# Opening of a two-layer diffusion block: small parameters ahead of X, squares on two engines, their sums on TensorE

## The chip, the cores and the metric

The kernel runs on one core of a Trainium2 chip. TensorE (PE; its weight loads are listed as PEld), VectorE (DVE), ScalarE (ACT) and GpSimd (POOL) each work through an instruction list of their own; SyncE (SP) issues the transfers. The metric is device microseconds of one execution; three executions of the kernel before took 1885.79, 1888.84 and 1891.24 us, so 1888.84 in the median.

## What is computed

A backbone of two layers over 512 latent tokens with 256 context tokens, width 1024. Layer 0 mixes tokens with grouped-query attention, layer 1 with a bidirectional Mamba-2 scan, and each is followed by a gated convolutional FFN. Each sub-layer starts like this (`c` conditions the latent tokens, `c_ctx` the context):

```python
silu_c = jax.nn.silu(c)
mod_l = jnp.split((silu_c @ ada_w[i] + ada_b[i])[:, None, :], 6, axis=-1)
# rms_norm(x, g) = x * rsqrt(mean(x * x, -1) + EPS) * g
h_l = rms_norm(x, norm_mix_w[i]) * (1 + mod_l[1]) + mod_l[0]
q_l, k_l, v_l = jnp.split(h_l @ w_qkv, [Q_DIM, Q_DIM + KV_DIM], axis=-1)
```

The change touches only the first of these, layer 0 ahead of attention: the silu of `c`, the sum of squares of every token, and the first products with `w_qkv`.

## The kernel before

X is kept with the width on the partitions: 8 row blocks (m = 0 to 7) of 128 x 512 latent columns and 128 x 256 context columns. A product of f32 exactness is made of three products of two-part operands (`mm3`, L105, L106, L108: high weights by high input, high by low, low by high). PE therefore needs for each block m a weight slab (`wst`, cast to `wsh` by ACT and reduced to the low part `wsl` by POOL) and a modulated input in two parts (`hha` by ACT, `hla` by DVE, both from `ht`).

The order on PE, ACT and DVE is the written order of the function `attention` (a manual schedule); SP issues in written order too. A transfer can be issued only when one of eight places is free.

The opening, in the names of the profile:

- `body` issues four transfers of X (L1562, two blocks each) and then all parameters (`par`, 548 columns, L1563). `attention` issues the weights of the first modulation (`wada`, in `ada`, L123, three transfers for each m), the slab (L544), the constants `cst` (L553) and so on up to m = 4.
- `busy(n)` makes n products of a matrix of ones with itself (`warm`, L565); nothing reads them.
- ACT squares the eight blocks (`sql`, L571), DVE adds them up in `acc` (L573), and `rstd_rows` lets PE sum over the partitions with four one-column products (`ssa`, L275), then makes the reciprocal root on DVE and ACT (`rsa` L279, `rsy` L281, `rsu` L283 and L284, `rba` L287) and turns it round on PE (`rsTa`, L293).
- `ada` of block m has three parts: issue the weights; eight products of the silu by the weights (`ps_ada`, L129) and their copy to SBUF (`ada_sb`, L131); two products that turn that copy round (`ps_adt`, L135) and the modulation on DVE (`mod` L146, `moda` L149). `modulated` then makes `ht` (L322), `hha` (L331) and `hla` (L332).
- The main loop runs over m. For each m there are six output groups (`k_step`, j = 0 to 5), three products each, into six PSUM accumulators `ps_l`. Within the groups of block m the second part of ada for m + 1 comes ahead of j = 0, its third part and the modulated input of m + 1 after j = 1. For m = 1 and 2 ACT squares four context blocks each and DVE adds them (`sqc`, L612 and L614).

Of the kernel before, what the change touches and what calls it, by code (L numbers as in the profile page):

```python
# [28 lines left out]
PC = {}  # L29
_n = 0  # L30


def _col(name, n):
    global _n
    PC[name] = _n
    _n += n


for _i in range(2):
    _col(f"nmix{_i}", KT)  # L40
    _col(f"nffn{_i}", KT)
    _col(f"adab{_i}", 6 * KT)
    for _t in range(3):
        _col(f"fw{_i}{_t}", NFT)
    _col(f"fb{_i}", NFT)
# [4 lines left out]
_col("snw", 16)  # L50
_col("alog", 1)
_col("dtb", 1)
_col("cc", 2 * KT)
_col("qn", 1)
_col("kn", 1)
NPAR = _n

CST_IDENT, CST_BLK, CST_SEL, CST_COS, CST_SIN = 0, 128, 130, 132, 132 + L
# [9 lines left out]
def t3(g, name, dt=F32, n=T):  # L68
    return g.t3p.tile([P, n], dt, tag="t3", bufs=g.n3, name=name)


def t4(g, name, dt=F32):
    return g.p.tile([P, 1024], dt, tag="t4", bufs=10, name=name)
# [35 lines left out]
    return i  # L109


def ada(g, src, layer, chunks, m0, nm, big=True):


    nc = g.nc
    cols = nm * len(chunks) * P
    per = (1024 if big else T) // cols
    st = []
    for k0 in range(0, KT, per):
        n = min(per, KT - k0)  # L120
        t = t4(g, "wada") if big else t3(g, "wada")
        t = t[:, : n * cols].rearrange("p (k a b) -> p k a b", k=n, a=len(chunks))
        nc.sync.dma_start(t.rearrange("p k a b -> p (k a b)"), src[:, k0 * cols : (k0 + n) * cols])  # L123
        st += [t[:, k].rearrange("p a b -> p (a b)") for k in range(n)]
    yield 0
    ps = Bank(g, "ps_ada")
    for k in range(KT):
        j = k % 4
        nc.tensor.matmul(ps[32 * j : 32 * j + 32, 0:cols], g.sc32[:, k, :], st[k], start=k < 4, stop=k >= 4)  # L129
    sb = g.t3p.tile([P, 512], F32, tag="t2", bufs=6, name="ada_sb")  # L130
    nc.vector.tensor_copy(sb[:, 0:cols], ps[:, 0:cols])  # L131
    yield BREAK
    pt = Bank(g, "ps_adt")
    for i in range(cols // P):
        nc.tensor.matmul(pt[:, 2 * i : 2 * i + 2], sb[:, i * P : (i + 1) * P], g.sel, start=True, stop=True)  # L135
    for i, ch in enumerate(chunks):
        modulation(g, pt[:, 2 * nm * i : 2 * nm * (i + 1)].rearrange("p (m v) -> p m v", v=2), layer, ch, m0, nm)
    yield BREAK
# [124 lines left out]
    follow(g, g.nc.scalar.preload_act_table_set("natural_log_exp_and_others"))  # L263


def rstd_rows(g, sq, n, cols, width, name, bank, behind=lambda: None):

    nc = g.nc  # L270
    c = cols.shape[-1]
    nt = n // P
    ps = bank(f"ss{name}")
    for t in range(nt):
        i = nc.tensor.matmul(ps[:, t * c : (t + 1) * c], sq[:, t * P : (t + 1) * P], cols, start=True, stop=True)  # L275
        ordered(g, i, behind())
    small = lambda nm: g.p.tile([P, nt * c], F32, tag="rst", bufs=8, name=nm)
    a, y, u = small("rsa"), small("rsy"), small("rsu")
    nc.vector.tensor_scalar(a, ps[:, : nt * c], 1.0 / width, EPS, ALU.mult, ALU.add)  # L279

    for f in ((lambda: nc.scalar.activation(y, a, AF.Ln)), (lambda: nc.scalar.activation(y, y, AF.Exp, scale=-0.5))):  # L281
        follow(g, f()) if g.tables else f()
    nc.vector.tensor_tensor(u, y, a, ALU.mult)  # L283
    nc.vector.scalar_tensor_tensor(u, y, -0.5, u, ALU.mult, ALU.mult)  # L284
    rb = t3(g, f"rb{name}", n=n)
    wide = lambda v: v.unsqueeze(2).broadcast_to([P, nt * c, P // c])
    nc.vector.scalar_tensor_tensor(rb.rearrange("p (a b) -> p a b", b=P // c), wide(u), 1.5, wide(y), ALU.add, ALU.mult)  # L287
    yield BREAK
    out = []
    for t0 in range(0, nt, 4):  # L290
        pt = bank(f"rsT{name}")
        for t in range(t0, min(nt, t0 + 4)):
            i = nc.tensor.transpose(pt[:, (t - t0) * P : (t - t0 + 1) * P], rb[:, t * P : (t + 1) * P], g.ident)  # L293
            ordered(g, i, behind())
        yield (pt, t0 * P, min(n, (t0 + 4) * P))
# [55 lines left out]
def Bank(g, name):  # L351
    return g.ps.tile([P, 512], F32, tag="B", bufs=4, name=name)
# [159 lines left out]
def attention(g, adas, project, X):  # L512


    nc, I = g.nc, g.I
    S64 = slice(0, 64), slice(64, 128)
    Bk, Sb = (lambda name: Bank(g, name)), (lambda name: S(g, name))
    t2 = lambda name, dt=F32: g.t3p.tile([P, 512], dt, tag="t2", bufs=6, name=name)
# [4 lines left out]
    ET = mybir.EngineType  # L523
    man = g.tc.manual_schedule(engines={ET.PE, ET.Activation, ET.DVE})
    man.__enter__()
    mods = [ada(g, I["adaA"][m], 0, (0, 1), m, 1, big=False) for m in range(KT)]
    W6 = 6 * P

    slabs = []
# [18 lines left out]

    loads = [slab() for _ in range(KT)]
    xs = [[X[:, m, c0:c1] for m in range(KT)] for c0, c1 in ((0, L), (L, T))]  # L550
    next(mods[0])
    next(loads[0])
    nc.sync.dma_start(g.cst, I["cst"][:, :CST_COS])  # L553
    for m in range(1, 5):
# [8 lines left out]
    def busy(n):  # L563
        for _ in range(n):
            nc.tensor.matmul(warm[:, :P], g.ones, g.ones, start=True, stop=True)  # L565

    busy(38)
    acc = t3(g, "acc", n=L)
    for m in range(KT):
        sq = t2("sql") if m else acc  # L570
        nc.scalar.activation(sq, xs[0][m], AF.Square)  # L571
        if m:
            nc.vector.tensor_tensor(acc, acc, sq, ALU.add)  # L573
    norm = rstd_rows(g, acc, L, g.ones[:, :1], D, "a", Bk)
    g.qn8 = g.const.tile([P, 1], F32, name="qn8")
    nc.vector.tensor_scalar(g.qn8, g.par[:, PC["qn"] : PC["qn"] + 1], -0.5 / HD * HD ** -0.5, None, ALU.mult)
    kn = g.const.tile([P, 1], F32, name="kn")
    nc.vector.tensor_scalar(kn, g.par[:, PC["kn"] : PC["kn"] + 1], -0.5 / HD, None, ALU.mult)

    e = g.p.tile([P, 2 * KT], F32, name="silu")  # L580
    nc.scalar.activation(e, g.cin, AF.Exp, scale=-1.0)
    nc.vector.tensor_scalar(e, e, 1.0, None, ALU.add)
    nc.vector.reciprocal(e, e)
    nc.vector.tensor_tensor(g.sc32[:, :, 0:2], g.cin.rearrange("p (k v) -> p k v", v=2),
                            e.rearrange("p (k v) -> p k v", v=2), ALU.mult)
    next(norm)
    next(mods[0])
    busy(8)
    rsl, _, _ = next(norm)
    next(mods[0])  # L590
    next(loads[0], None)
    busy(3)
    modulated(g, hl[0], xs[0], rsl, 0, L, 0, 1, 0, 0, 0)
    rs_ps, rsl = rsl, t3(g, "rsl", n=L)
# [8 lines left out]
    for m in range(KT):  # L603
        if 1 <= m < KT - 5 + 1:
            next(mods[m + 5 - 1])
            next(loads[m + 5 - 1])
        if m == 1:
            sqc = t3(g, "sqc", n=C)
        if m in (1, 2):
            for a in range(4 * m - 4, 4 * m):  # L610
                sq = t2("sqc")[:, :C] if a else sqc
                nc.scalar.activation(sq, xs[1][a], AF.Square)  # L612
                if a:
                    nc.vector.tensor_tensor(sqc, sqc, sq, ALU.add)  # L614
        if m == 3:
            norm = rstd_rows(g, sqc, C, g.ones[:, :1], D, "a", Bk)
            next(norm)
        if m == 4:
            rsc = t3(g, "rsc", n=C)
            pt, _, _ = next(norm)  # L620
            nc.scalar.copy(rsc, pt[:, :C])
        for j in range(6):
            if m + 1 < KT and j == 0:
                next(mods[m + 1])
            k_step(m, j, pl[j], hl)
            if m + 1 < KT:
                if j == 0:
                    next(loads[m + 1], None)
                if j == 0 + 1:
                    next(mods[m + 1])  # L630
                    modulated(g, hl[m + 1], xs[0], rsl, 0, L, 0, 1, 0, 0, m + 1)
            if m >= 4 and j == 1:
                for a in (2 * m - 8, 2 * m - 7):
                    modulated(g, hc[a], xs[1], rsc, 0, C, 0, 1, 0, 1, a, pool=True)
# [221 lines left out]
    for n, j in enumerate((0, 1, 2, 4, 5, 3)):  # L856
        ps = Bk("ps_c")
# [67 lines left out]
    a = [ada_job(gen) for gen in adas]  # L925
# [27 lines left out]
    m = pairs[0].maxima()  # L953
# [12 lines left out]
    for p in range(NH // 2):  # L966
        m = iter(())
        if p < 7:
# [3 lines left out]
            m = pairs[p + 1].maxima()  # L972
# [570 lines left out]
def body(nc, tc, I, out, dbg=None):  # L1543
    g = Ctx()
# [7 lines left out]
    X = pool("x", phx).tile([P, KT, T], F32, name="X")  # L1552
# [4 lines left out]
    cst = g.cst = g.const.tile([P, CST_COS], F32, name="cst")  # L1557
    g.cs = g.t3p.tile([P, 2 * L], F32, name="cs")
    g.cos, g.sin = g.cs[:, :L], g.cs[:, L:]
    g.par = g.const.tile([P, NPAR], F32, name="par")  # L1560
    for m in range(0, KT, 2):
        nc.sync.dma_start(X[:, m : m + 2, :L], I["xT"][m * P : (m + 2) * P].rearrange("(k p) t -> p k t", p=P))  # L1562
    nc.sync.dma_start(g.par, I["par"])  # L1563
    g.ident, g.blk, g.sel = (cst[:, a:b] for a, b in
                             ((CST_IDENT, CST_IDENT + P), (CST_BLK, CST_BLK + 2), (CST_SEL, CST_SEL + 2)))
    g.ones = g.const.tile([P, P], F32, name="ones")
# [158 lines left out]
```

## Time and profile before

| | us |
|---|---|
| median of three executions | 1888.84 |
| profiled execution | 1887.32 |
| its span, first to last instruction | 1885.5 |
| PE busy | 1858.7 |
| first product of warming | 1.05 |
| first product of the main loop | 18.85 |
| first product of m = 1, of m = 2 | 25.24, 31.08 |

A row of the timeline has the start, the time until the last of the merged instructions ended, the engine, the line, the operation with output and inputs, the count, and in brackets the idle time before it and what ended that. Ends of products on PE are modelled: the next product starts before the one before is shown to end. All times are counted from the first instruction.

### The profile page before, as it was taken

The page shows a single profiled execution, that of the slowest core. Times are in us where ns is not written, and L with a number is a line of the kernel's source. Part 1 is how long each engine was busy: PE and PEld are TensorE (multiplying, and loading weights), DVE is VectorE, ACT ScalarE, POOL GpSimd, SP SyncE. Part 2 cuts the span into 40 slices and gives each one's busy share as a digit, 9 for nine tenths or more (in the row PEclk, how much of TensorE's full clock was granted, in tenths as well). Part 3 has the DMA queues.
Part 4 walks back from the last instruction along what each step waited for, and adds up shares of the span by engine and source line. Part 5 has one row for each costly group of instructions (what it writes and reads, how often), then busy time and mean ns, then how long its engine had stood idle before and what let it go on. Part 6 is the DMA issues. An engine that isn't in the chain of part 4 may idle for free.

```text
span 1885.5 us, 27465 instructions
## 1 busy us (share of the span) xinstructions
PE 1858.7 (99%) x10794; PEld 1531.4 (81%) x10794; DVE 1347.4 (71%) x2013; ACT 833.0 (44%) x1422; POOL 256.2 (14%) x220
## 2 busy tenths in 40 slices
PE   9999999999999999999999999999999999999999
PEld 7865555689888888888888888888888888888887
DVE  5688999678777777444478977777888576565655
ACT  3655544354222222222257577776666352323331
POOL 2100000030000000000031235554434100000000
PEclk9999999999999999999999999999999999999999
DMA  9223241015443554222224244344344323323232
GB/s 342 74 79 113 89 145 62 7 62 177 147 130 119 174 185 153 68 68 68 67 79 140 69 122 135 113 122 123 112 141 118 100 78 102 101 86 104 90 101 90
DMA packets 73489, 210.02 MB, mean 111 GB/s; under 512 B 8976, under 2 KB 14480, under 8 KB 73232
## 3 DMA queue, kind: packets, MB, share of 16 engines
q1 hardware_dynamic: 73360, 208.26, 35.0%
q8 instruction: 85, 1.39, 0.3%
q14 instruction: 44, 0.36, 0.1%
HBM read 198.79 MB, written 6.82 MB: 109 GB/s over the span
## 4 chain that ended last, share of the span: by engine, by line
PE 83%; DVE 10%; DMA 2%; issue 2%; ACT 2%; POOL 0%; SPq 0%; DVEq 0%; ACTq 0%; POOLq 0%
PE ps_up L105 10%; PE ps_up L106 10%; PE ps_up L108 10%; PE ps_d L105 6%; PE ps_d L108 6%; PE ps_d L106 5%; PE ps_in L105 4%; PE ps_in L108 4%; PE ps_in L106 4%; PE ps_o L799 2%; PE ps_s L835 2%; PE ps_st L1340 2%; PE ps_wo L105 1%; PE ps_wo L106 1%; PE ps_wo L108 1%
## 5 line engine op out<-in xcount | busy, mean ns | idle before, releaser
L87 DVE TENSOR_TENSOR wl<-wst,wh 128x1024 fp32r<-128x1024 f32 x211 | 261.8, 1241 | 279.2 <-PE ps_up L106 122.5
L85 ACT CAST wh<-wst 128x1024 fp32r<-128x1024 f32 x211 | 221.0, 1048 | 441.7 <-DMA wst<-in_wup 309.4
L106 PE MATMUL ps_up<-hlf,wh 128*128 128x512 f32 x992 | 351.6, 354 | 0.0
L108 PE MATMUL ps_up<-hhf,wl 128*128 128x512 f32 x992 | 351.4, 354 | 0.0
L105 PE MATMUL ps_up<-hhf,wh 128*128 128x512 f32 x992 | 351.2, 355 | 0.0
L105 PEld LDWEIGHTS ps_up<-hhf,wh 128*128 128x128 f32 x992 | 187.5, 189 | 26.2
L106 PEld LDWEIGHTS ps_up<-hlf,wh 128*128 128x128 f32 x992 | 187.6, 189 | 26.0
L108 PEld LDWEIGHTS ps_up<-hhf,wl 128*128 128x128 f32 x992 | 187.4, 189 | 26.2
L105 PE MATMUL ps_in<-hhs,wh 128*128 128x512 f32 (+1 forms) x544 | 199.5, 367 | 0.0
L108 PE MATMUL ps_in<-hhs,wl 128*128 128x512 f32 (+1 forms) x544 | 193.6, 356 | 0.0
L106 PE MATMUL ps_in<-hls,wh 128*128 128x512 f32 (+1 forms) x544 | 193.3, 355 | 0.0
L108 PE MATMUL ps_d<-hdh,wl 128*128 128x512 f32 (+1 forms) x496 | 173.4, 350 | 0.0
L105 PE MATMUL ps_d<-hdh,wh 128*128 128x512 f32 (+1 forms) x496 | 173.3, 350 | 0.1
L106 PE MATMUL ps_d<-hdl,wh 128*128 128x512 f32 (+1 forms) x496 | 172.9, 349 | 0.0
L1022 DVE SCALAR_TENSOR_TENSOR X<-ps_d,mod,X 128x256 f32<-128x256 f32 (+1 forms) x176 | 102.4, 611 | 27.0 <-PE ps_d L108 26.8
L108 PEld LDWEIGHTS ps_in<-hhs,wl 128*128 128x128 f32 x544 | 102.7, 189 | 14.9
L105 PEld LDWEIGHTS ps_in<-hhs,wh 128*128 128x128 f32 x544 | 102.9, 189 | 14.3 <-issue 1.2
L106 PEld LDWEIGHTS ps_in<-hls,wh 128*128 128x128 f32 x544 | 103.0, 189 | 13.0
L106 PEld LDWEIGHTS ps_d<-hdl,wh 128*128 128x128 f32 x496 | 93.2, 188 | 14.4 <-DVE hdl L87 0.2
L108 PEld LDWEIGHTS ps_d<-hdh,wl 128*128 128x128 f32 x496 | 93.1, 188 | 13.1
L105 PEld LDWEIGHTS ps_d<-hdh,wh 128*128 128x128 f32 x496 | 93.0, 188 | 13.0 <-ACT hdh L85 0.3
L168 DVE SCALAR_TENSOR_TENSOR junk<-wada,cb 128x1024 f32<-128x1024 f32 x80 | 97.1, 1214 | 1.1 <-ACT cb L159 0.8
(375 smaller groups left out, 3654.0 us busy)
## 6 DMA issues: line engine op xcount, KB each, us to landing
wst<-in_wup SPq DMA_DIRECT2D x88, 512.0 KB, 3.6
wada<-in_adaT SPq DMA_DIRECT2D x56, 512.0 KB, 3.7
wst<-in_win SPq DMA_DIRECT2D x48, 512.0 KB, 3.6
wst<-in_wdown SPq DMA_DIRECT2D x44, 512.0 KB, 3.7
E<-ad SPq DMA_DIRECT2D x64, 256.0 KB, 7.1
wada<-in_adaB SPq DMA_DIRECT2D x24, 512.0 KB, 4.7
ec<-ead SPq DMA_DIRECT2D x64, 128.0 KB, 4.3
wst<-in_wout SPq DMA_DIRECT2D x16, 512.0 KB, 3.5
```

The lines of the kernel that those rows point to most:

```text
L85: keep(nc.scalar.copy(hi, src))
L87: keep(eng.tensor_tensor(lo, src, _r(hi), ALU.subtract))
L105: mm(out, wh, ah, start=first, stop=False)
L106: mm(out, wh, al, start=False, stop=False)
L108: i = mm(out, wl, ah, start=False, stop=last)
L168: g.tc.keep_in_program_order(nc.vector.scalar_tensor_tensor(junk, w, 1.0, cb[:, v * D : (v + 1) * D], ALU.mult, ALU.mult, accum_out=md[:, ...
L799: nc.tensor.matmul(po[S64[e], :n], v, pr[:, 512 * e + off : 512 * e + off + n], start=first, stop=last)
L835: nc.tensor.matmul(outs[e], a[S64[e], k], b[S64[e], q], start=i == 0, stop=False)
L1022: nc.vector.scalar_tensor_tensor(ap, o[:, c0:c1], gate[:, m, v : v + 1], ap, ALU.mult, ALU.add)
L1340: nc.tensor.matmul(ps[:, d * 256 : (d + 1) * 256], Bt[:, t * P : (t + 1) * P], xw[d][t], start=t == ts[0], stop=t == ts[-1])
```

## The change

Seven edits, all in the opening:

1. The parameters are ordered anew, so that the 74 columns that the opening needs come first (`c` and `c_ctx`, the norm weights and the modulation biases of layer 0, the q and k gains). They are the first transfer; the other 474 columns follow after the slab of m = 1.
2. X comes in eight transfers of one block, with `cst` after the fourth.
3. The silu is computed at once, ahead of the squares.
4. ACT squares the even blocks and DVE the odd ones; DVE's adds are gone, and PE sums every block into one accumulator with four one-column products a block (32 in place of 4).
5. Warming products: 38 become 10, the 8 ahead of the transposes go, and 3 come between the sums and ada of m = 0; the 3 ahead of the first main product stay.
6. The copy `ada_sb` of m = 0 goes from DVE to ACT.
7. In block m = 0 the second part of ada of m = 1 comes ahead of j = 2 in place of j = 0, and its third part after j = 3 in place of j = 1. So it now stands among the main products.

```diff
+    nc.sync.dma_start(g.par[:, :NFIRST], I["par"][:, :NFIRST])
-    for m in range(0, KT, 2):
-        nc.sync.dma_start(X[:, m : m + 2, :L], I["xT"][m * P : (m + 2) * P].rearrange("(k p) t -> p k t", p=P))
-    nc.sync.dma_start(g.par, I["par"])
+    for m in range(KT):
+        nc.sync.dma_start(X[:, m, :L], I["xT"][m * P : (m + 1) * P])
+        if m == 3:
+            nc.sync.dma_start(g.cst, I["cst"][:, :CST_COS])
...
-    busy(38)
-    acc = t3(g, "acc", n=L)
-    for m in range(KT):
-        sq = t2("sql") if m else acc
-        nc.scalar.activation(sq, xs[0][m], AF.Square)
-        if m:
-            nc.vector.tensor_tensor(acc, acc, sq, ALU.add)
-    norm = rstd_rows(g, acc, L, g.ones[:, :1], D, "a", Bk)
...
+    busy(10)
+    ss = Bk("ssa")
+    for m in range(KT):
+        sq = t2("sql")
+        if m % 2:
+            nc.vector.tensor_tensor(sq, xs[0][m], xs[0][m], ALU.mult)
+        else:
+            nc.scalar.activation(sq, xs[0][m], AF.Square)
+        for t in range(L // P):
+            nc.tensor.matmul(ss[:, t : t + 1], sq[:, t * P : (t + 1) * P], g.ones[:, :1],
+                             start=m == t == 0, stop=m == KT - 1 and t == L // P - 1)
+    norm = rstd_rows(g, None, L, g.ones[:, :1], D, "a", Bk, ps=ss)
     next(norm)
+    busy(3)
     next(mods[0])
-    busy(8)
+    next(loads[0], None)
     rsl, _, _ = next(norm)
     next(mods[0])
-    next(loads[0], None)
     busy(3)
...
         for j in range(6):
-            if m + 1 < KT and j == 0:
+            j0 = 0 if m else 2
+            if m + 1 < KT and j == j0:
                 next(mods[m + 1])
             k_step(m, j, pl[j], hl)
             if m + 1 < KT:
-                if j == 0:
+                if j == j0:
                     next(loads[m + 1], None)
-                if j == 0 + 1:
+                if j == j0 + 1:
                     next(mods[m + 1])
                     modulated(g, hl[m + 1], xs[0], rsl, 0, L, 0, 1, 0, 0, m + 1)
```

PE's list from its start to the second part of ada of m = 1, before (`hha`, `hla` with their block's number; line numbers are those of each kernel's own file):

```order
L565 MATMUL warm<-ones 128x128 x38
L275 MATMUL ssa<-ones,acc 128x1 x4
L129 MATMUL ps_ada<-wada,sc_83 32x256 x8
L565 MATMUL warm<-ones 128x128 x8
L293 MATMUL rsTa<-cst,rba 128x128 x4
L135 MATMUL ps_adt<-cst,ada_sb 128x2 x2
L565 MATMUL warm<-ones 128x128 x3
L129 MATMUL ps_ada<-wada,sc_83 32x256 x8
L105 MATMUL ps_l<-hha_0_102,wsh 128x512
```

The same place in the changed kernel:

```order
L569 MATMUL warm<-ones 128x128 x10
L591 MATMUL ssa<-ones,sql 128x1 x32
L569 MATMUL warm<-ones 128x128 x3
L133 MATMUL ps_ada<-wada,sc_88 32x256 x8
L298 MATMUL rsTa<-cst,rba 128x128 x4
L139 MATMUL ps_adt<-cst,ada_sb 128x2 x2
L569 MATMUL warm<-ones 128x128 x3
L109 MATMUL ps_l<-hha_0_107,wsh 128x512
L110 MATMUL ps_l<-hla_0_108,wsh 128x512
L112 MATMUL ps_l<-hha_0_107,wsl 128x512
L109 MATMUL ps_l<-hha_0_107,wsh 128x512
L110 MATMUL ps_l<-hla_0_108,wsh 128x512
```

The 28 warming products that are gone are as many as the sums that came; ada of m = 1 no longer stands ahead of the first main product (it follows after one more product).

ScalarE's list from its start to the first modulated input, before:

```order
L571 ACTIVATE acc<-X 128x512
L571 ACTIVATE sql<-X 128x512 x7
L581 ACTIVATE silu<-par 128x16
L281 ACTIVATE rsy<-rsa 128x4
L281 ACTIVATE rsy<-rsy 128x4
L85 CAST wsh<-wst 128x768
L331 ACTIVATE hha_0_102<-ht,mod_86 128x512
```

And in the changed kernel:

```order
L572 ACTIVATE silu<-par 128x16
L589 ACTIVATE sql<-X 128x512 x4
L286 ACTIVATE rsy<-rsa 128x4
L286 ACTIVATE rsy<-rsy 128x4
L135 COPY ada_sb<-ps_ada 128x256
L89 CAST wsh<-wst 128x768
L336 ACTIVATE hha_0_107<-ht,mod_91 128x512
```

The silu stands first, four squares are gone to VectorE, and the copy of ada stands between the root and the cast of the first slab. Beyond the opening every engine's list is the same in both kernels.

More of the change, by code (lines that the diff above doesn't have):

```diff
@@ L36, in _col @@
     _n += n
+_col("cc", 2 * KT)
+_col("nmix0", KT)
+_col("adab0", 6 * KT)
+_col("qn", 1)
+_col("kn", 1)
+NFIRST = _n
 for _i in range(2):
-    _col(f"nmix{_i}", KT)
+    if _i:
+        _col("nmix1", KT)
+        _col("adab1", 6 * KT)
     _col(f"nffn{_i}", KT)
-    _col(f"adab{_i}", 6 * KT)
     for _t in range(3):
@@ L52 @@
 _col("dtb", 1)
-_col("cc", 2 * KT)
-_col("qn", 1)
-_col("kn", 1)
 NPAR = _n
@@ L109, in mm3, with ada @@
     return i
-def ada(g, src, layer, chunks, m0, nm, big=True):
+def ada(g, src, layer, chunks, m0, nm, big=True, copy=None):
     nc = g.nc
@@ L130, in ada @@
     sb = g.t3p.tile([P, 512], F32, tag="t2", bufs=6, name="ada_sb")
-    nc.vector.tensor_copy(sb[:, 0:cols], ps[:, 0:cols])
+    (copy or nc.vector.tensor_copy)(sb[:, 0:cols], ps[:, 0:cols])
     yield BREAK
@@ L263, in ln_exp, with rstd_rows @@
     follow(g, g.nc.scalar.preload_act_table_set("natural_log_exp_and_others"))
-def rstd_rows(g, sq, n, cols, width, name, bank, behind=lambda: None):
+def rstd_rows(g, sq, n, cols, width, name, bank, behind=lambda: None, ps=None):
     nc = g.nc
@@ L272, in rstd_rows @@
     nt = n // P
-    ps = bank(f"ss{name}")
-    for t in range(nt):
+    sums = ps is None
+    ps = bank(f"ss{name}") if sums else ps
+    for t in range(nt) if sums else ():
         i = nc.tensor.matmul(ps[:, t * c : (t + 1) * c], sq[:, t * P : (t + 1) * P], cols, start=True, stop=True)
@@ L525, in attention @@
     man.__enter__()
-    mods = [ada(g, I["adaA"][m], 0, (0, 1), m, 1, big=False) for m in range(KT)]
+    mods = [ada(g, I["adaA"][m], 0, (0, 1), m, 1, big=False, copy=None if m else nc.scalar.copy) for m in range(KT)]
     W6 = 6 * P
@@ L550, in attention @@
     xs = [[X[:, m, c0:c1] for m in range(KT)] for c0, c1 in ((0, L), (L, T))]
[L551 to L554, printed above, removed]
+    for m in range(5):
         next(mods[m])
         next(loads[m])
+        if m == 1:
+            nc.sync.dma_start(g.par[:, NFIRST:], I["par"][:, NFIRST:])
         if m == 2:
@@ L565, in busy @@
             nc.tensor.matmul(warm[:, :P], g.ones, g.ones, start=True, stop=True)
-    busy(38)
-    acc = t3(g, "acc", n=L)
-    for m in range(KT):
-        sq = t2("sql") if m else acc
-        nc.scalar.activation(sq, xs[0][m], AF.Square)
-        if m:
-            nc.vector.tensor_tensor(acc, acc, sq, ALU.add)
-    norm = rstd_rows(g, acc, L, g.ones[:, :1], D, "a", Bk)
[L575 to L578, printed above, removed]
     e = g.p.tile([P, 2 * KT], F32, name="silu")
@@ L585, in attention @@
                             e.rearrange("p (k v) -> p k v", v=2), ALU.mult)
+    g.qn8 = g.const.tile([P, 1], F32, name="qn8")
+    nc.vector.tensor_scalar(g.qn8, g.par[:, PC["qn"] : PC["qn"] + 1], -0.5 / HD * HD ** -0.5, None, ALU.mult)
+    kn = g.const.tile([P, 1], F32, name="kn")
+    nc.vector.tensor_scalar(kn, g.par[:, PC["kn"] : PC["kn"] + 1], -0.5 / HD, None, ALU.mult)
+    busy(10)
[10 more added lines that the diff above has]
+    norm = rstd_rows(g, None, L, g.ones[:, :1], D, "a", Bk, ps=ss)
     next(norm)
+    busy(3)
     next(mods[0])
-    busy(8)
+    next(loads[0], None)
     rsl, _, _ = next(norm)
     next(mods[0])
-    next(loads[0], None)
     busy(3)
```

## The prediction

> **What bounds the kernel now.** I read the page first, then the timeline of the opening engine by engine, then windows around the places where TensorE's rate changes. From the page:
>
> ```profile
> span 1885.5 us, 27465 instructions
> PE 1858.7 (99%) x10794; PEld 1531.4 (81%) x10794; DVE 1347.4 (71%) x2013; ACT 833.0 (44%) x1422; POOL 256.2 (14%) x220
> ```
>
> TensorE (PE) is busy for all but 27 us, so whatever moves the first main product, and adds no work behind it, moves the end. But the busy time counts warming products too, so the opening has to be read by itself:
>
> ```profile
> 1.05 10.57 PE L565 MATMUL warm<-ones 128*128 128x128 f32 x76 [1.05 <-DVE ones L1567]
> 11.99 1.05 PE L275 MATMUL ssa<-ones,acc 128*128 128x1 f32 x8 [0.36 <-DVE acc L573]
> 12.97 1.07 PE L129 MATMUL ps_ada<-wada,sc 128*32 128x256 f32 x16
> 13.97 2.05 PE L565 MATMUL warm<-ones 128*128 128x128 f32 x16
> 15.86 0.60 PE L293 MATMUL rsTa<-cst,rba 128*128 128x128 f32 x4
> 16.30 0.51 PE L135 MATMUL ps_adt<-cst,ada_sb 128*128 128x2 f32 x4
> 17.51 1.07 PE L129 MATMUL ps_ada<-wada,sc 128*32 128x256 f32 x16
> 18.85 0.50 PE L105 MATMUL ps_l<-hha,wsh 128*128 128x512 f32 x1 [0.27 <-ACT hha L331]
> 19.64 0.50 PE L106 MATMUL ps_l<-hla,wsh 128*128 128x512 f32 x1 [0.29 <-DVE hla L332]
> 20.91 0.50 PE L135 MATMUL ps_adt<-cst,ada_sb 128*128 128x2 f32 x4
> 23.92 0.39 PE L108 MATMUL ps_l<-hha,wsl 128*128 128x512 f32 x1
> 24.24 1.07 PE L129 MATMUL ps_ada<-wada,sc 128*32 128x256 f32 x16
> 25.24 0.50 PE L105 MATMUL ps_l<-hha,wsh 128*128 128x512 f32 x1
> 26.75 0.50 PE L135 MATMUL ps_adt<-cst,ada_sb 128*128 128x2 f32 x4
> ```
>
> The first main product starts at 18.85. A product of f32 leaves two records (38 warming products, x76). Beside these rows, on VectorE (DVE) and ScalarE (ACT):
>
> ```profile
> 9.55 1.15 ACT L571 ACTIVATE sql<-X 128x512 f32<-128x512 f32 x2 [0.21 <-DMA X<-in_xT]
> 8.86 3.08 DVE L573 TENSOR_TENSOR acc<-acc,sql 128x512 f32<-128x512 f32 x4 [0.47 <-ACT sql L571]
> 13.08 0.16 DVE L279 TENSOR_SCALAR rsa<-ssa 128x4 f32<-128x4 f32 x1 [0.44 <-PE ssa L275]
> 14.14 0.76 DVE L287 SCALAR_TENSOR_TENSOR rba<-rsu,rsy 128x512 f32<-128x512 f32 x1
> 14.83 0.41 DVE L131 COPY ada_sb<-ps_ada 128x256 f32<-128x256 f32 x1
> 13.90 0.83 ACT L85 CAST wsh<-wst 128x768 fp32r<-128x768 f32 x1 [0.18 <-DMA wst<-in_wslab]
> 15.09 1.81 POOL L87 TENSOR_TENSOR wsl<-wst,wsh 128x768 fp32r<-128x768 f32 x1
> 17.30 0.75 DVE L322 SCALAR_TENSOR_TENSOR ht<-X,moda,rsTa 128x512 f32<-128x512 f32 x1
> 18.08 0.72 ACT L331 ACTIVATE hha<-ht,mod 128x512 fp32r<-128x512 f32 x1 [3.34 <-DVE ht L322]
> ```
>
> The chain to 18.85 is: X lands (last pair 9.5), squares, seven adds on DVE until 11.94, the sums on PE until 13.04, the reciprocal root until 14.90, then the transposes, which sit behind eight warming products until 15.86, then the second part of ada (16.30), the modulation, ht, hha.
>
> **The rate of PE.** The windows view (length, then busy time and records of PE and PEld, in the longer rows of DVE, ACT and POOL too, then granted clock, DMA share, GB/s), first of the warming products alone, then around the one place inside the kernel where the granted clock falls, and behind them what PE did there:
>
> ```profile
> 1.42:4.84 3.42, 3.42 (x18) 3.42 (x17) 1.00 0.77 256
> 4.98:11.35 6.37, 6.37 (x59) 6.37 (x58) 1.00 0.99 350
> 1448.74:1452.15 3.41, 1.42 (x11) 1.00 (x9) 1.79 (x2) 2.90 (x5) 1.27 (x1) 1.00 0.47 147
> 1452.15:1455.57 3.42, 3.42 (x11) 2.74 (x11) 3.04 (x6) 3.33 (x7) 0.00 (x0) 0.50 0.03 10
> 1455.57:1458.98 3.41, 3.41 (x16) 2.77 (x15) 2.32 (x5) 1.61 (x3) 0.00 (x0) 1.00 0.00 0
> 182.41:185.82 3.41, 2.02 (x14) 0.96 (x11) 2.30 (x5) 3.35 (x6) 0.00 (x0) 1.00 0.17 67
> ...
> 1451.34 1.15 PE L275 MATMUL ssy<-ones,ysq 128*128 128x1 f32 x8 [1.99 <-POOL ysq L1430]
> ```
>
> A count takes in records that only reach into the window, one or two each. So a record takes about 3.42 / 16 = 0.21 us until 4.9 and 6.37 / 57 = 0.11 after it: PE starts at half rate and doubles 3.9 us after its first product. In the third window it is busy for 1.42 of 3.41 us (42%), with 2 us of idle time ahead of eight one-column records (the last row), and the next window is at clock 0.50 and lets through 11 records where the one behind it has 16. A window with 2.02 of 3.41 us (59%) kept the clock. The eight records of the sums above take 0.91 us from first start to the next product's room (11.99 to about 12.90), so 0.11 each: a product of one column costs a record as much as one of 128.
>
> **The change, part by part.** *PE until the sums end.* Before: 76 + 8 = 84 records. After: 10 warming products and 32 sums, 20 + 64 = 84 records. The adds leave DVE, but the stream on PE keeps its length; what goes is the wait for acc. The 77th record could start at 1.05 + 10.57 less the pipelined end, about 11.45, and starts at 11.99: gain 0.5 us (0.4 by the idle time in its row). The sums then end at 12.5, not 13.04. That holds if no block of X comes late: PE reaches block m at 5.2 + 0.9 m, the last at 11.5. X's last pair landed at 9.5; as tenth issue of about 0.46 us each, the last block goes out at 0.74 + 9 x 0.46 = 4.9, and landing takes 4.1 to 7.3 us here:
>
> ```profile
> L1562 SPq DMA_DIRECT2D X<-in_xT x4: 437/464/469, 0.7 to 2.2; - x4
> DMA to landing us min/median/max: 4.1/6.9/9.1
> wada<-in_adaA SPq DMA_DIRECT2D x1, 256.0 KB, 8.6
> ```
>
> The 7.3 is of the fourth 512 KB of X, with three ahead. The bytes ahead of the last block grow only by 74 parameter columns and 132 of cst (206 x 4 B x 128 rows, 0.1 MB), so I take 9.5 again; its square on DVE costs at most an add (0.77), so 10.3, and cover of 1.2 us. Split squares, early silu and small parameters are therefore hidden by PE's stream: I cost them at nothing. If that cover went (X at 10.7 or later), each us more is a us.
>
> *From the sums to the first product.* The root keeps its operations: 14.90 - 13.04 = 1.86, so 14.4. Meanwhile PE runs 3 warming products (0.7) and ada of m = 0 (1.0), from 12.4 to 14.2; its last weights were issued near 4.4, took 8.6 us (the third row above) and landed near 13.0, and now have 0.17 MB less ahead (206 columns for 548). Its copy, now on ACT, is bounded by DVE's 0.41 from below and hha's 0.72 (twice the columns) from above; 0.45 makes 14.7. The transposes need no longer wait behind eight warming products: 14.4 to 14.85. So the second part of ada starts at 14.85 instead of 16.30, 1.45 us earlier, and with the same 2.55 us behind it (18.85 - 16.30) the first main product at 17.4. The slab's cast wsh comes after the copy (0.83, to 15.6) and GpSimd's wsl behind it (1.81, to 17.4), for the third product at about 18.4: hidden by 1 us.
>
> *Behind the first product.* Ada of m = 1 stood in the idle stretch ahead of the first product (17.51). Now it stands after six products, on the path. Its price is that of m = 2: from the last product's start 23.92 to the next at 25.24 is 1.32, less 0.23 for a product: 1.09 us. So the gain is 1.45 - 1.09 = 0.36 when its second part runs, at 20.91 + 2 x 0.7 - 0.36 = 21.95, two output groups later than before. What it feeds is then late:
>
> ```profile
> 22.81 0.72 ACT L331 ACTIVATE hha<-ht,mod 128x512 fp32r<-128x512 f32 x1 [2.80 <-DVE ht L322]
> 23.57 0.75 DVE L332 SCALAR_TENSOR_TENSOR hla<-ht,mod,hha 128x512 fp32r<-128x512 f32 x1 [0.79 <-ACT hha L331]
> 24.64 1.48 DVE L614 TENSOR_TENSOR sqc<-sqc 128x256 f32<-128x256 f32 x3 [0.32 <-ACT sqc L612]
> 26.04 0.42 DVE L131 COPY ada_sb<-ps_ada 128x256 f32<-128x256 f32 x1
> 33.96 0.61 PE L135 MATMUL ps_adt<-cst,ada_sb 128*128 128x2 f32 x4 [1.21 <-DVE ada_sb L131]
> ```
>
> hla of m = 1 ended 24.32 - 20.91 = 3.41 us after ada's second part began; so now at 25.35. PE wants it after 0.36 + 1.4 + 1.09 + 0.23 = 3.1 us: a wait of 0.3. Behind hla on DVE stand three adds of context squares (1.48) and the copy for m = 2 (0.42): they end at 27.25, while PE, six products and that wait after 24.8, wants the copy's result at about 26.55: a wait of 0.7, where before there was none (the copy ended at 26.46, PE came at 26.75). Then 27.25 stands against 26.75: 0.5 us late. From there the order is the old one and the 1.21 us wait of the next stage comes again, shifted. The sum: -1.45 + 1.09 + 0.3 + 0.7 = +0.6, or +0.5 read off the two times; bounds -1.4 (both waits and ada vanish in slack) and +2 (wada or the cast half a us late at two places).
>
> The profiled execution took 1887.32 us, 1.8 around its span, and lies 1.5 below the median of 1888.84. So 1887.8 for an execution like it, and **1889.3 us** against the median. 0.3% is 5.7 us, about what a measurement here can tell from no change.
>
> **The rivals.** *The clock falls during the sums (slower).* The stretch from 5.2 to 12.4 would hold nothing but one-column products. For it: the window that lost the clock held eight records of this very form and they did not save it; by moving columns that window was nearly empty. Against: by busy time it had 42%, the new stretch has 100%, and 59% was enough. It decides from the point where a window of 3.4 us holds sums alone. Price: 64 records at 0.21 for 0.11 are 6.4 us, 4.8 if one window of 16 records still runs full; ada, warming and adt twice as long with 1.6 us of it not hidden by the root; one or two windows of main products at 11 records for 16, 1.2 us each; less the two waits of 0.5. Together +7 to +10: 1896 to 1899.
> [...]
>
> *The clock falls ahead of the first product.* After ada's second part and three warming products PE idles from about 15.9 to 17.4, and twice 0.3 around it; a window that starts near 14.8 is about half busy, between 42% and 59%. For it, that; against, main products fill the rest of most placings. Price 1.2 us on top: 1890.5.
>
> *The gain stays.* If DVE's adds and hla slip into slack, the first product's 1.45 us remain: 1887.4. Against: DVE does these in a written order. (That the split of the squares itself changes nothing is part of the forecast: PE paces the sums.)
>
> **How the numbers follow.** Forecast 0.48, the fall in the sums 0.33, the fall ahead of the first product 0.08, the kept gain 0.11. Nothing in the opening gives 5.7 us back; 0.04 for faster by measurement alone. Slower by over 0.3% is the first rival, 0.32 after its mildest end; the rest, 0.64, is within. The range takes in the forecast with the spread of the runs, from 1886, and most of the first rival, to 1898; the forecast's own range is 1886.5 to 1891.5.
>
> **What would show it.** Sums ending near 12.5 with records 0.11 apart; the first main product near 17.4; ada of m = 1 between main products; new waits of PE for hla and for ada_sb before 28 us; m = 2 starting about 0.5 us late. Clock 0.50 anywhere between 5 and 20 us, or sums 0.21 apart, and I am wrong; so too if X's blocks, not PE, set the pace of the sums.

## The result and the profile after

| | before | after |
|---|---|---|
| median of five executions, us | 1888.84 (1885.79 to 1891.24) | 1896.98 (1896.55 to 1900.30) |
| profiled execution, us | 1887.32 | 1896.58 |
| its span, us | 1885.5 | 1894.8 |
| sums of the squares end, about | 13.04 | 17.58 |
| first product of the main loop | 18.85 | 25.68 |
| first product of m = 2 | 31.08 | 42.18 |

The ratio is 1.0053, with a 95% interval from 1.0041 to 1.0065: some 10 us slower. That is the first rival, not the forecast. One execution of the kernel before among those timed beside the experiments took 3042.68 us at a mean granted clock of 0.555 and is left out of the ratios and of the counts below. From the page of the kernel after:

```profile
span 1894.8 us, 27439 instructions
PE 1865.3 (98%) x10784; PEld 1535.7 (81%) x10784; DVE 1345.7 (71%) x2009; ACT 831.8 (44%) x1419; POOL 256.0 (14%) x220
...
PEclk7999999999999999999999999999999999999999
```

TensorE has ten instructions fewer and 6.6 us more busy time, so its instructions became slower. The clock row is 7 in the first slice, and a slice is 47 us. In the page of the kernel before it is 9 in all forty slices:

```profile
PEclk9999999999999999999999999999999999999999
```

The opening on TensorE, in the timeline of the kernel after:

```profile
1.05 4.01 PE L569 MATMUL warm<-ones 128*128 128x128 f32 x20 [1.05 <-DVE ones L1578]
4.90 1.84 PE L591 MATMUL ssa<-ones,sql 128*128 128x1 f32 x16
7.39 10.19 PE L591 MATMUL ssa<-ones,sql 128*128 128x1 f32 x48 [0.65 <-ACT sql L589]
17.45 1.63 PE L569 MATMUL warm<-ones 128*128 128x128 f32 x6
19.00 1.94 PE L133 MATMUL ps_ada<-wada,sc 128*32 128x256 f32 x16
20.87 0.85 PE L298 MATMUL rsTa<-cst,rba 128*128 128x128 f32 x4
21.56 0.51 PE L139 MATMUL ps_adt<-cst,ada_sb 128*128 128x2 f32 x4
21.92 0.91 PE L569 MATMUL warm<-ones 128*128 128x128 f32 x6
25.68 0.80 PE L109 MATMUL ps_l<-hha,wsh 128*128 128x512 f32 x1 [2.85 <-ACT hha L336]
```

The last 48 records of the sums take 10.19 us, 0.21 each; the 16 before them 1.84, 0.11 each. The same halving of the rate shows in ada (1.94 for 16 records, before 1.07). The windows of the kernel after, cut where the granted clock changes (length, busy time and records of PE, PEld, DVE, ACT and POOL, granted clock, DMA share, GB/s):

```profile
4.25:7.66 3.41, 2.76 (x26) 2.67 (x25) 0.97 (x2) 0.99 (x2) 0.04 (x1) 1.00 0.96 324
7.66:21.31 13.65, 13.65 (x72) 12.16 (x72) 2.99 (x7) 1.95 (x6) 0.75 (x2) 0.50 1.02 378
21.31:24.73 3.42, 1.53 (x14) 1.33 (x12) 2.56 (x4) 0.82 (x2) 1.80 (x1) 1.00 1.09 362
24.73:31.55 6.82, 5.87 (x24) 3.07 (x25) 1.32 (x3) 1.93 (x3) 1.83 (x1) 0.50 1.04 398
```

The clock falls behind the first stretch that holds mostly sums, and stays at 0.50 for 13.65 us in which TensorE is busy without a break. It comes back at 21.31, after products of 256 and 128 columns have run, and falls again behind a stretch with 45% busy time, ahead of the first product. Every stretch is a multiple of 3.41 us long.

The path by places: the sums end 4.5 us later, the first product starts 6.8 later, m = 2 starts 11.1 later, m = 3 at 49.91 for 38.74, 11.2 later. From there to the end 1.9 us come back. Most of that has one place, which the instructions of the sums behind the layers show (duration in ns, minimum, median and maximum, then first and last start); before:

```profile
L275 PE MATMUL ssy<-ones,ysq x8: 250/250/350, 1451.3 to 1452.1; 128*128 128x1 f32 x8
L275 PE MATMUL ssf<-ones,sqf x8: 250/250/271, 1516.5 to 1522.4; 128*128 128x1 f32 x8
```

and after:

```profile
L280 PE MATMUL ssy<-ones,ysq x8: 250/250/271, 1462.0 to 1462.8; 128*128 128x1 f32 x8
L280 PE MATMUL ssf<-ones,sqf x8: 250/250/271, 1525.4 to 1531.4; 128*128 128x1 f32 x8
```

`ssy` is 10.7 us later than before and `ssf` 8.9. Between them lies the place where the profiled execution of the kernel before lost its clock, at 1452.15; the one after did not lose it there. The 1.99 us of idle time ahead of `ssy` stand in both profiles (ahead of 1451.34 and of 1461.96), and the change edits nothing there, so the difference is put down to the execution and not to the change (more under the last heading).

A second thing that the prediction had not seen stands on VectorE and GpSimd, in the timeline of the kernel after:

```profile
22.27 1.80 POOL L91 TENSOR_TENSOR wsl<-wst,wsh 128x768 fp32r<-128x768 f32 x1 [13.82 <-ACT wsh L89]
22.36 1.73 DVE L153 SCALAR_TENSOR_TENSOR moda<-mod,par 128x2 f32<-128x2 f32 x1
24.13 0.75 DVE L327 SCALAR_TENSOR_TENSOR ht<-X,moda,rsTa 128x512 f32<-128x512 f32 x1
```

`moda`, an operation on two columns, takes 1.73 us and ends at 24.09, when GpSimd's low part of the slab ends (24.07). It is on the path to the first product, which now starts 4.12 us after ada's last part (21.56 to 25.68) and not 2.55.

### The profile page after: what moved, and what is told of

It is laid out like the page before. It is cut to its first block, busy times and chain, and to the rows that moved or that the text cites. A ratio compares the mean times of both kernels' runs of the same rounds, so it can differ in the third digit from the quotient of the medians.

```text
span 1894.8 us, 27439 instructions
## 1 busy us (share of the span) xinstructions
PE 1865.3 (98%) x10784; PEld 1535.7 (81%) x10784; DVE 1345.7 (71%) x2009; ACT 831.8 (44%) x1419; POOL 256.0 (14%) x220
## 4 chain that ended last, share of the span: by engine, by line
PE 82%; DVE 8%; DMA 4%; ACT 2%; issue 2%; SPq 1%; POOL 0%; DVEq 0%; POOLq 0%; ACTq 0%
PE ps_up L109 10%; PE ps_up L110 10%; PE ps_up L112 10%; PE ps_d L109 6%; PE ps_d L112 5%; PE ps_d L110 5%; PE ps_in L109 4%; PE ps_in L112 4%; PE ps_in L110 4%; PE ps_o L808 2%; PE ps_st L1349 2%; PE ps_s L844 2%; PE ps_wo L110 1%; PE ps_wo L109 1%; PE ps_wo L112 1%
```

## The experiments

Two theories of the fall in the sums. **A**: what holds the clock is columns streamed, not the time that records fill; one-column products do not hold it. **B**: the sums wait for X and its squares (0.65 us ahead of 7.39; the window that lost the clock was 81% busy), and the gaps lose it.

**The sums 128 columns wide.** The weights stay the square of X; all 128 columns of ones are streamed where one was, and one column of the result is used.

```diff
-    nc.tensor.matmul(ss[:, t : t + 1], sq[:, t * P : (t + 1) * P], g.ones[:, :1], ...)
+    nc.tensor.matmul(ss[:, t * P : t * P + 128], sq[:, t * P : (t + 1) * P], g.ones[:, :128], ...)
```

> Each of the 32 sums multiplies by 128 columns of ones instead of one; one column of each result is used. Weight loads, squares, transfers and order are those of the change, and a record of a product takes 0.11 us at full clock for 1 or for 128 columns. Theory A (the clock is granted by the columns that move through the array, and one-column sums move none): granted clock 1.00 from about 4.5 us through the whole opening, sums 0.11 us a record, ending near 12.9 with the squares as they land now (last at 11.05), first main product at 17.8, or up to 19.4 if the modulation still waits behind GpSimd's low part as it does in the changed kernel (1.73 us); time within 1 to 2 us of the kernel before, so 1888 to 1891 where before takes 1889. Theory B (PE lost the clock because it waits for blocks of X, 0.65 us at 7.39, with too few warming products ahead): the waits are the same, so the clock falls to 0.50 again near 8 us, sums end near 17.6, and the time is that of the change, 1896 to 1900.

Measured: 1892.41 for 1888.20, ratio 1.0023 [1.0014, 1.0032]. Its timeline and its windows:

```profile
5.48 7.66 PE L591 MATMUL ssa<-ones,sql 128*128 128x128 f32 x64
12.98 0.83 PE L569 MATMUL warm<-ones 128*128 128x128 f32 x6
15.48 0.51 PE L139 MATMUL ps_adt<-cst,ada_sb 128*128 128x2 f32 x4
16.29 1.68 DVE L153 SCALAR_TENSOR_TENSOR moda<-mod,par 128x2 f32<-128x2 f32 x1
19.56 0.55 PE L109 MATMUL ps_l<-hha,wsh 128*128 128x512 f32 x1 [2.79 <-ACT hha L336]
```

```profile
9.63:13.05 3.42, 3.42 (x33) 3.42 (x32) 0.69 (x1) 0.34 (x1) 0.00 (x0) 1.00 0.97 326
16.46:19.87 3.41, 0.62 (x4) 0.30 (x2) 2.59 (x3) 1.09 (x2) 1.49 (x1) 1.00 1.04 392
19.87:23.28 3.41, 3.17 (x14) 1.77 (x17) 0.42 (x1) 0.84 (x2) 1.83 (x1) 0.50 1.06 373
```

The 64 records start within 7.5 us, 0.12 each, although each streams 128 columns, and the clock stays at 1.00 through the sums. The mean granted clock of the five executions of the change is 0.993 to 0.995, of the eleven here 0.996 to 0.998. So 0.30% of the time, 5.7 us, is the fall in the sums, and what is left is 0.23%. Part of that is in the rows: `moda` takes 1.68 us here too, and the long idle time that it leaves (a window with 18% busy time) comes just before the clock falls to 0.50, at 19.87. The row of the sums has no wait for a square either, so this run alone does not tell A from B.

**The change with 38 warming products in place of 10.** By the profile after, where the last block of X landed at 10.3, X has then arrived before the first sum (here at 11.00).

```diff
-    busy(10)
+    busy(38)
```

> The changed kernel with 38 warming products ahead of the sums instead of 10, so that all blocks of X have been squared (11.05) when the first sum starts at about 11.5, and the 64 records of one column run without a wait. Theory A: a window of 3.4 us that holds sums alone still ends in clock 0.50, so the sums take 8.5 to 11 us instead of 7.2, end between 20 and 22.5, and the time is 6 to 12 us over the kernel before. Theory B: no wait, 38 warming products, so the clock stays at 1.00, the sums end at 18.8, the first main product comes near 23.7, and the time is about 5 us over the kernel before.

Measured in one execution: 1905.58 for 1888.20. Timeline and windows:

```profile
11.00 10.76 PE L591 MATMUL ssa<-ones,sql 128*128 128x1 f32 x64
```

```profile
10.77:14.18 3.41, 3.41 (x34) 3.41 (x32) 0.69 (x1) 0.63 (x1) 0.00 (x0) 1.00 1.01 322
14.18:34.66 20.48, 18.91 (x95) 14.70 (x94) 4.07 (x9) 3.44 (x7) 3.64 (x2) 0.50 1.04 391
```

No wait stands in the row, the window that ends at 14.18 is 100% busy by its records, and the clock falls behind it. B cannot explain that. A does, but its size was missed: 17.4 us over the kernel before, where 6 to 12 were expected. The sums end at 21.76, as expected, and the clock then stays at 0.50 for 12.9 us more, through ada and the first main products. Why it came back so late is not shown. (One square on ScalarE, 0.63 us, and one on VectorE, 0.69 us, ran within this window and so not by 11.05; they held nothing up.)

**How many columns it takes: 32 and 64.** The same edit with 32 or 64 columns of ones. Under A there is a width between 1 and 128 columns from which on the clock holds.

> [...] Theory B expects the fall whatever the width.

> [...] 32 columns lost the clock, 128 kept it. If the clock is granted by moving columns there is a bound between, and this run falls on one side of it: clock 1.00 to about 17 us and sums ending near 13, or 0.50 from about 8 us and sums ending near 17.6.

Measured in one execution each: 1897.14 (before 1888.20) with 32, 1892.28 (before 1888.67) with 64. The row of the sums and two windows of the kernel with 32 columns, and behind them windows of the one with 64:

```profile
7.53 10.45 PE L591 MATMUL ssa<-ones,sql 128*128 128x32 f32 x48 [0.85 <-ACT sql L589]
...
7.46:10.87 3.41, 3.34 (x16) 3.35 (x16) 1.77 (x3) 1.27 (x3) 0.79 (x2) 0.50 1.00 345
10.87:14.29 3.42, 3.42 (x18) 3.42 (x17) 0.31 (x1) 0.00 (x0) 0.00 (x0) 0.50 1.01 364
```

```profile
6.75:10.16 3.41, 3.41 (x32) 3.41 (x32) 1.39 (x2) 1.69 (x3) 0.79 (x2) 1.00 1.02 351
10.16:13.58 3.42, 3.42 (x33) 3.42 (x33) 0.85 (x2) 0.19 (x2) 0.00 (x0) 1.00 1.02 382
```

With 32 columns it is the case of one column, 16 records in a window at clock 0.50; with 64 the clock is kept, at 32 records. The sizes of the weights, the count of products and their order are the same in both. One thing more differs: with 32 columns TensorE waited 0.85 us for a square, in the window that lost the clock (4.05 to 7.46, 77% busy), and with 64 it did not wait. The wait alone does not explain the loss: a window of wider products (256 and 512 columns, 182.41 to 185.82) kept the clock with 59% in the kernel before, and the window from 10.87, 100% busy with 32-column products, did not bring the clock back. So in these two runs products of 32 columns, 100% busy by their records, stayed at clock 0.50, and 64 columns were enough to hold 1.00 in a stream of f32 products 0.11 us apart. A finer step was not run, nor 32 columns without a wait, and whether the columns streamed or the results written for them count is not separated.

**The transfers and the early silu alone.** Edits 1 to 3 of the change, with the warming products, squares, adds and sums of before, the copy on VectorE and ada of m = 1 in its old place.

> Only the transfers and the silu of the change: small parameters first, X in eight transfers, cst after the fourth, silu ahead of the squares; squares on ScalarE, adds on VectorE, warming products, copy and the place of ada of m = 1 as before. Both theories: the clock stays at 1.00 as before. The last block of X landed at 10.36 in the changed kernel and at 9.5 before, in pairs; the last add then ends near 11.75 instead of 11.94, and the eight warming products behind hold the transposes anyway: first main product within 0.4 us of 18.85, time within 1 us of the kernel before. A rival: the early X blocks come late enough to move it by more than 1 us.

Measured: 1888.73 for 1888.20, ratio 1.0007 [0.9997, 1.0017]. They cost nothing that can be measured, and bring nothing.

**Where the remaining 0.23% goes.** All three kernels below keep the wide sums. The first casts slab 0 on ScalarE ahead of ada's copy, so that GpSimd would be done before `moda`; the second puts ada of m = 1 back ahead of j = 0; the third does both.

```diff
 # the cast first
     busy(3)
-    next(mods[0])
     next(loads[0], None)
+    next(mods[0])
 # ada of m = 1 back
-            j0 = 0 if m else 2
+            j0 = 0
```

> The run with 128-column sums, with the cast of the first slab ahead of the copy of ada of m = 0 on ScalarE (two lines change places). Theory: VectorE's moda takes 1.68 us in place of 0.16 because it cannot finish while GpSimd makes the slab's low part (16.15 to 17.95 there); with the cast at about 13.9 the low part runs from about 14.8 to 16.6, moda ends at 16.6 and the first main product comes at 18.1 instead of 19.56. The idle stretch of PE ahead of it shrinks from 2.8 to about 1.4 us, so the clock falls there in fewer executions. Time 1.4 to 2.6 us below the 128-column run: about 1890. Rival (the 1.68 us have another cause, such as the copy or the transfer of the parameters): moda stays long and nothing changes.

Measured: 1892.12 for 1888.67, ratio 1.0021 [1.0012, 1.0029], so next to no gain on 1.0023. In its timeline GpSimd still stands beside `moda`:

```profile
15.81 1.80 POOL L91 TENSOR_TENSOR wsl<-wst,wsh 128x768 fp32r<-128x768 f32 x1 [7.98 <-ACT wsh L89]
16.90 0.73 DVE L153 SCALAR_TENSOR_TENSOR moda<-mod,par 128x2 f32<-128x2 f32 x1
```

The slab lands only near 14.8 in this order of transfers, so the cast could not run at 13.9 as before. `moda` again ends with GpSimd (17.63 and 17.61), and ada's copy, now behind the cast, came later: most of what one won, the other lost (first product at 19.22 for 19.56).

> The 128-column run with only the second part of ada of m = 1 back ahead of the first main product, and its third part after j = 1 in place of j = 3. By the prediction's sum the move costs 1.09 us of PE and two waits of 0.3 to 0.7 us: here the first main product stays near 19.6, m = 1 starts 6.4 us behind it (before: 6.39) instead of 7.6, no wait of PE for the copy of m = 2 is left, and the time is 1.3 to 2 us below the 128-column run, more where the clock no longer falls in the idle stretch that ada now fills by 1.1 us. Rival: the move costs nothing, since PE waits elsewhere anyway, and the time is the same.

Measured: 1888.66 for 1888.67, ratio 1.0005 [0.9995, 1.0014]. From 1.0023 to 1.0005 are some 3.4 us for one line, with each end uncertain by 0.001. Even so the clock is not always saved: in the profiled execution, the longest of the twelve (1894.92), `moda` takes 1.70 us, TensorE still waits ahead of its first product, and behind a window with 41% busy time the clock is 0.50 for 6.83 us.

```profile
19.98 0.49 PE L109 MATMUL ps_l<-hha,wsh 128*128 128x512 f32 x1 [1.81 <-ACT hha L336]
```

> Both repairs on the 128-column run: cast ahead of the copy, and the second part of ada of m = 1 back ahead of the first main product, its third part after j = 1. If the three causes are all there is (columns that move nothing, moda behind the low part, ada on the path), the first main product comes at 18.1, with ada of m = 1 in the idle stretch ahead of it, m = 1 starts at 24.5 against 25.24 before, m = 2 at 30.3 against 31.08, the clock stays at 1.00 through the opening, and the time is 0 to 1 us below the kernel before: ratio 0.9995 with an interval that takes in 1. Rival (something else in the change costs time): ratio over 1.001.

Measured: 1890.15 for 1888.67, ratio 1.0006 [0.9997, 1.0014]: the same as without the cast.

**The move of ada alone, in the kernel before.**

```diff
         for j in range(6):
-            if m + 1 < KT and j == 0:
+            j0 = 0 if m else 2
+            if m + 1 < KT and j == j0:
...
-                if j == 0:
+                if j == j0:
                     next(loads[m + 1], None)
-                if j == 0 + 1:
+                if j == j0 + 1:
```

> The kernel before with one edit: ada of m = 1 among the main products of m = 0 (second part ahead of j = 2, third after j = 3), as in the change. The prediction's terms, here alone: 1.09 us of PE on the path, a wait of 0.3 us for hla of m = 1 and one of up to 0.7 us for the copy of m = 2, so the first product stays at 18.85, m = 1 starts near 26.4 to 26.7 and m = 2 near 33, and the time is 1.5 to 2 us over the kernel before: ratio 1.0008 to 1.0011, perhaps more where the idle 1.4 us that it leaves ahead of the first product lets the clock fall. Rival: it is hidden, ratio 1.000.

Measured: 1891.17 for 1888.19, ratio 1.0014 [1.0003, 1.0026]: 2.6 us, with an interval from 0.6 to 4.9. Timeline and windows:

```profile
18.89 0.50 PE L105 MATMUL ps_l<-hha,wsh 128*128 128x512 f32 x1 [1.28 <-ACT hha L331]
...
21.89 1.77 PE L129 MATMUL ps_ada<-wada,sc 128*32 128x256 f32 x16
...
30.22 0.61 PE L135 MATMUL ps_adt<-cst,ada_sb 128*128 128x2 f32 x4 [0.30 <-DVE ada_sb L131]
```

```profile
16.54:19.95 3.41, 1.85 (x11) 1.34 (x11) 1.89 (x5) 1.83 (x3) 0.33 (x1) 1.00 1.02 391
19.95:23.37 3.42, 3.42 (x21) 1.60 (x20) 0.00 (x0) 0.09 (x1) 1.82 (x1) 0.50 1.08 359
```

The first product comes no earlier than before (18.89, before 18.85), so this is the bare price. Ada now stands in the path, the wait for the copy of m = 2 is 0.30, and the place that ada left ahead of the first product is idle: 54% busy in that window, and the next one at clock 0.50.

**The collision of VectorE and GpSimd taken away.** Wide sums, ada of m = 1 back, and the low part of slab 0 made by VectorE between `ht` and `hla` instead of by GpSimd.

```diff
-    split(g, st, hi, lo, lo_engine="pool" if k < 7 else "dve")
+    if k:
+        split(g, st, hi, lo, lo_engine="pool" if k < 7 else "dve")
+        return
+    nc.scalar.copy(hi, st)
+    g.low0 = lambda: nc.vector.tensor_tensor(lo, st, _r(hi), ALU.subtract)   # called behind ht
```

> 128-column sums, ada of m = 1 back ahead of the first main product, and the low part of the first slab made by VectorE between ht and hla instead of by GpSimd. If moda was long because GpSimd made that low part at the same time, moda now takes 0.16 us, ht starts about 0.4 us after ada's second part ends, and the first main product comes 2.55 us after that part starts, at about 18.0 (before: 18.85; the 128-column run: 19.56); hla is 0.2 us later than hha by more (the low part takes about 0.96), so the second product waits about 1 us instead of 0.3. m = 1 starts near 24.6 against 25.24. Time equal to the kernel before or up to 1 us below: ratio 0.999 to 1.000. Rival (moda is long for another reason): moda stays at 1.7 us and the first product at 19.6 or later.

Measured: 1888.06 for 1888.19, ratio 0.9997 [0.9989, 1.0006]. Its timeline:

```profile
15.14 0.51 PE L139 MATMUL ps_adt<-cst,ada_sb 128*128 128x2 f32 x4
15.94 0.16 DVE L153 SCALAR_TENSOR_TENSOR moda<-mod,par 128x2 f32<-128x2 f32 x1
16.80 0.95 DVE L557 TENSOR_TENSOR wsl<-wst,wsh 128x768 fp32r<-128x768 f32 x1
17.69 0.50 PE L109 MATMUL ps_l<-hha,wsh 128*128 128x512 f32 x1
```

`moda` is back at 0.16, and the first product starts 2.55 us after ada's last part, at 17.69: 1.16 earlier than in the kernel before. Still the time is that of before.

**The wait of the stage m = 2.** The 1.21 us for which TensorE waits for the copy of ada of m = 3 came again in all of these (1.31 in the kernel above, at 34.04). Two kernels give that copy to ScalarE: the one above, and the kernel before.

```diff
-    mods = [ada(..., copy=None if m else nc.scalar.copy) for m in range(KT)]
+    mods = [ada(..., copy=nc.scalar.copy if m in (0, 3) else None) for m in range(KT)]
 # in the kernel before: nc.scalar.copy if m == 3 else None
```

> The run with the low part on VectorE, and the copy of ada of m = 3 moved to ScalarE. That copy stands behind four adds on VectorE, one of which takes 1.9 us while GpSimd works, and PE waits 1.2 to 1.3 us for it in every run so far. If that wait is on the path, m = 3 starts 1.2 us earlier, fewer executions lose the clock in that wait, and the time is 1 to 2.5 us below the kernel before: ratio 0.9987 to 0.9995. Rival (the wait comes back further on, at the modulation behind the same adds): m = 3 starts as late as without it, ratio 0.9995 to 1.0005.

> The kernel before with only the copy of ada of m = 3 on ScalarE. Same theory: PE's wait of 1.21 us at 33.96 goes, m = 3 starts at 37.5 instead of 38.74, ratio 0.9990 to 0.9995. Rival: the wait comes back behind the modulation, ratio 1.000.

Measured: 1886.95 for 1888.19, ratio 0.9994 [0.9984, 1.0004], and 1885.55 for 1888.19, ratio 0.9990 [0.9978, 1.0002]. In the kernel before with that copy alone the wait is gone, and m = 3 starts at 37.43 for 38.74, as expected:

```profile
26.81 0.61 PE L135 MATMUL ps_adt<-cst,ada_sb 128*128 128x2 f32 x4 [0.51 <-DVE ada_sb L131]
...
32.76 0.50 PE L135 MATMUL ps_adt<-cst,ada_sb 128*128 128x2 f32 x4
```

In the row for m = 2 a wait of 0.51 appears that the profile of the kernel before does not have; with the low part on VectorE it is 1.44. The second kernel has the lowest median of all, but both intervals hold 1, and so it is not shown to be faster.

## Why the prediction was wrong, point by point

**The step that failed** is the weighing of the first rival, the sentence "by busy time it had 42%, the new stretch has 100%, and 59% was enough". It took the busy time of records as what holds the clock, and so put the cost of the fall at nothing in the forecast. The run with 38 warming products has a window 100% busy with one-column products and loses the clock behind it; the run with 32 columns was at 0.50 in a window 100% busy, those with 64 and 128 kept 1.00 in the sums. The row of before that hinted at this was quoted, eight one-column records in the window that lost the clock, but with 42% busy time that row could not decide. So the busy time of records alone does not hold the clock; the runs show this for products with 1 and 32 columns.

**The rival's mechanism held, its total in part by luck.** It gave +7 to +10; the profile shows +9.3, the medians +8.1. But the wide sums alone give back 5.7 us, and part of the rest is `moda`'s collision, which it had not in its sum. Of its two prices for the sums the smaller came, 4.8 if one window of 16 records still runs full: they end 5.1 us after the 12.5 of the forecast, 4.5 after those of before, since the first 16 records kept the full rate. Its "from the point where a window of 3.4 us holds sums alone" was too late: the window 4.25 to 7.66 held some warming products and was enough.

**The terms of the forecast**, as far as runs with the clock held show them:

- *The sums at TensorE's pace, 0.11 a record, end at 12.5.* Nearly: in the runs with 128 columns the product behind the sums starts between 12.41 and 13.38. The last block of X landed at 10.3 in the profile after and not at 9.5.
- *The root 1.86, then 2.55 from ada's last part to the first product at 17.4.* Right where nothing disturbs it: 15.14 and 17.69 with the low part on VectorE. In the change itself the term for `moda` was mis-sized: it was put at 0.16 and took 1.73.
- *The cast and GpSimd's low part "hidden by 1 us".* Wrong: the step looked at who waits for the result (the third product) and not at who runs beside it. It even put GpSimd at 15.6 to 17.4, which is where the modulation stands. The trace of before had the sign. Of `moda` and of an add of context squares it has these instructions (ns, minimum, median and maximum):

```profile
L149 DVE SCALAR_TENSOR_TENSOR moda<-mod,par x12: 151/162/1610, 17.1 to 710.4; 128x2 f32<-128x2 f32 x8, 128x8 f32<-128x8 f32 x3, 128x16 f32<-128x16 f32 x1
...
L614 DVE TENSOR_TENSOR sqc<-sqc x4: 418/425/1870, 30.1 to 31.7; 128x256 f32<-128x256 f32 x4
...
31.44 1.85 POOL L87 TENSOR_TENSOR wsl<-wst,wsh 128x768 fp32r<-128x768 f32 x1 [3.59 <-ACT wsh L85]
```

  The add that began at 31.7 took 1.87 us for 0.42, and GpSimd ran until 33.29. The `moda` of 1610 ns, again of two columns, began at 52.94 and ended at 54.55; GpSimd made a low part from 52.70 to 54.54. A maximum ten times the median asks for a reason. In the change and in the run with the cast first, too, `moda` ended within 0.02 us of GpSimd's low part. By what means the one holds up the other is not shown.
- *Ada of m = 1 on the path: 1.09, and waits of 0.3 and 0.7.* In sum +2.1; the move alone measured 2.6 [0.6, 4.9], which agrees, in a wide interval. Its make-up does not: the wait for the copy was 0.30, and the profile has a window at clock 0.50 besides (19.95 to 23.37).
- *The transfers, the early silu and the split squares at nothing.* No cost was measured for the first two, 1.0007 [0.9997, 1.0017]. The split was not run alone; it is in the kernel at 0.9997, with the copy on ScalarE.
- *From the stage of m = 3 on, the old order with the 1.21 us wait.* Right: the row at 45.13 of the kernel after has 1.28.

```profile
45.13 0.61 PE L139 MATMUL ps_adt<-cst,ada_sb 128*128 128x2 f32 x4 [1.28 <-DVE ada_sb L135]
```

**The clock ahead of the first product** had a chance of 0.08 as a rival of its own. It fell there in the profiles of the change, of the runs with 128, 64 and 32 columns, of the cast first, of ada back alone and of the move alone. The windows that lost it were 15% (64 columns) to 60% (32 columns) busy, so 59% was no safe bound here either; the one with 60% held no product of more than 256 columns. That the idle stretch grows when ada leaves it was seen, but not how little of the window ahead of the fall main products fill in these placings; with `moda` late it was less still (18% busy in all with 128 columns, 54% in the move alone).

Put together, the ratios fall in steps as the causes are taken away: 1.0053 as it is, 1.0023 with wide sums, 1.0005 with ada of m = 1 back, 0.9997 with the low part on VectorE. That is 5.7, 3.4 and 1.5 us; the intervals of neighbours touch in the last two, so these two sizes are rough. Why the last kernel, with its first product 1.16 us earlier, is not faster than before by more than 0.03% is explained in part by its wait for the copy of m = 2 (0.88 at 26.62); in its profile m = 2 starts at 31.06, before 31.08.

## What to carry to other kernels

Of a product that only fills TensorE's time, look at the columns that it streams as well as at its record: here 64 f32 columns held the clock at 1.00 and 32 were at 0.50, and a record with 128 columns took no longer than one with a single column, 0.11 us. An engine that looks hidden must be checked for who runs beside it as well as for who waits for it; the minimum and maximum of one operation in the trace of before show such a collision (0.15 and 1.61 us for `moda`). When filler is moved out of an idle stretch, the clock behind that stretch can be part of its price: in the kernel before with ada moved the window was 54% busy and the next one at 0.50.

## What the runs showed of the hardware

- *One-column f32 products did not hold the clock even without a gap*, and in the profiles here it came back only after wider products had run (at 21.31 in the change, where the sums end at 17.58). In the run with 38 warming products it was 0.50 for 20.48 us, 7.6 of them in the sums and 12.9 behind them.
- *In these profiles changes of the clock were multiples of 3.41 us apart, and their places differed from profile to profile.* They came at 7.66, 21.31, 24.73 and 31.55 in one profile, at 19.87 and 23.28 in another. Behind the gap of 1.99 us ahead of `ssy` a window went at 0.50 in the profile before (1452.15 to 1455.57) and none in the one after.
- *The granted clock goes with a good part of the kernel's own spread.* Of 86 executions of the kernel before timed beside the experiments, those with a mean granted clock of 1.000 have a median of 1885.3 us (9), of 0.999 1887.1 (24), of 0.998 1888.7 (40), of 0.997 1890.0 (13). 0.001 of the time is 1.9 us; 0.001 of the clock goes with about 1.6 us.
- *A VectorE operation on two columns took 1.73 us instead of 0.16 beside a GpSimd operation with which it shares no data*, and 0.16 again when VectorE made that low part itself.
